# Two blocks split ahead between two layers, rows normed on two engines, and a last norm that uses TensorE

## The chip, the cores and the metric

The kernel runs on one core of one Trainium2 chip. Its engines are TensorE (PE in the profile, with weight loads as PEld), VectorE (DVE), ScalarE (ACT), GpSimd (POOL) and SyncE (SP), which here only issues DMAs. The metric is the device time of one execution in microseconds, the median of several runs. All times below are in microseconds, counted from the start of the span.

## The reference, cut to what matters

Two layers over 256 tokens of width 2048: a Mamba-2 SSD layer, then a sparse-attention layer. After each, the residual is added and the rows are normed:

```python
def layer_norm(x, g, b):
    mu = mean(x, -1); var = mean((x - mu)**2, -1)
    return (x - mu) * rsqrt(var + 1e-5) * g + b

def ssd_mixer(x, w_in, ...):
    z, xbc, dt = split(x @ w_in)            # 4096, 4096 + 2048, 64 columns
    xs, bm, cm = split(silu(conv4(xbc)))    # 8 groups of 8 heads of 64
    y = ssd(xs, dt, a, bm, cm) + d_skip * xs
    yg = rms_norm_per_group(y * silu(z)) * norm_g
    return yg @ w_out

def dsa_mixer(x, w_in, ...):
    c_q, c_kv, k_idx, w_idx, gate = split(x @ w_in)   # 512, 256, 64, 16, 4096
    ...                                               # index scores, top 64, attention
    return (o * silu(gate)) @ w_out

x = layer_norm(4**0.25 * x + ssd_mixer(x), ln_g[0], ln_b[0])
x = layer_norm(4**0.25 * x + dsa_mixer(x), ln_g[1], ln_b[1])
```

## The kernel before

All weights stream from memory in 404 blocks of 128 x 1024 (eight of them 128 x 672). For each block, SyncE loads it into one of four `raw` buffers, ScalarE copies it to a rounded high part `hi` (L98), VectorE subtracts to get the low part `lo` (L106), and TensorE uses both, so that a product of full accuracy is made of fast reduced-precision passes. The class `Stream` (L65) keeps this list: `run` (L120) goes through the blocks, splits up to `SPLIT` = 4 blocks ahead (`convert_to`, L115), issues the block's products and then lets every running side job take one step (a job is a Python generator, a `yield` ends its step). `st.limit` caps how far ahead is split. `convert` with `later=True` (by way of `start`, L109) issues only ScalarE's high part; `finish` (L104) issues the low part and the load of the block four places on. Nothing reorders this: each engine works in the order in which the program issues to it, and waits by semaphores.

The first layer's input projection is 160 blocks, 20 for each of 8 groups; the last eight of a group make its four z tiles, each summed out of PSUM by `halves` (L289: ScalarE copies one half, VectorE adds the other, in two steps of a job) and gated in `z_steps` (L324). The sums take three PSUM buffers in turn (`acc_tile`), and the two halves of the first output block `o1_0` take the next two of them. `xst_steps` (L382) transposes a pair of x tiles on TensorE. Then the output projection follows: 64 blocks (`out_proj`, L495), block column by block column; of the last one the products of the second token half are held back for six blocks, and `tail1` (L997) places them.

Between the layers, for each half of 128 tokens: `residual` (L546) adds and takes statistics on VectorE, `normed` (L953) gets the mean and the inverse root in small steps (`rsqrt1_steps`, L201) and norms four quarters of 512 columns in place, `turn` (L975) transposes a quarter on TensorE, `put` (L982) scales it by gain and bias on ScalarE and splits it into `x1T`, which the next layer's first blocks (`wcq`, `stream_tok`, L630) read. Here `n_o1` is the first of those blocks; eight of them also hold back their second token half, and `early` (L1027) makes the second half's turns and puts behind the sixth and the seventh. `AHEAD` (L55) is how many of the new layer's blocks may be split before `tail1`.

At the end, `last` (L1094) places the held products of the final output block (their last 256 columns in `part`), then `residual2` and `normed2(0)` for the first token half, then the same for the second half: mean and root, and for each quarter `center` (subtract the mean, times the gain), `scale` (times the root, plus the bias) and a write to the output by SyncE.

Of the kernel before, what the change touches and what calls it, by code (L numbers as in the profile page):

```python
# [9 lines left out]
F32 = mybir.dt.float32  # L10
# [6 lines left out]
P = 128  # L17
# [34 lines left out]
EARLY = 8  # L52
HELD = 6
LAST = 8
AHEAD = 4  # L55


class Unit:
# [78 lines left out]
def trunk_kernel(ctx: ExitStack, tc: tile.TileContext, x, xt, w1, wdt, dtp, prm, wo1,  # L137
# [23 lines left out]
    def m_tile(name):  # L161
        return p_m.tile([P, 512], F32, tag="m", name=name)
# [48 lines left out]
    def now(gen):  # L211
        for _ in gen:
            pass
# [72 lines left out]
                                         skip_group_check=True)  # L286
        return pe

    def halves(dst, ps):  # L289
        nc.scalar.activation(dst, ps[:, T:2 * T], AF.Copy)  # L290
        yield
        v.tensor_add(dst, ps[:, 0:T], dst)  # L292
        yield

# [29 lines left out]
    def z_steps(g, ci, cell):  # L324
        ps = cell["ps"]
        zs = sp2.tile([P, T], F32, tag="zs", name=f"zs{g}_{ci}", bufs=4)
        yield from halves(zs, ps)
        th = sp3.tile([P, T], F32, tag="craw", name=f"zt{g}_{ci}")
        nc.scalar.activation(th, zs, AF.Tanh, scale=0.5)
        yield  # L330
        v.scalar_tensor_tensor(zs, th, 1.0, zs, op0=ALU.add, op1=ALU.mult)
        G[g][("z", ci)] = zs
        yield
# [226 lines left out]
    for g in range(NG):  # L560
        u = 20 * g
        gap = 5 if g < 7 else 2
        st.side(u + 9, (cb_steps, g))
        st.side(u + 13, (xst_steps, g, 0))
        st.side(u + 18, (xst_steps, g, 1))
        for c in range(4):
            st.side(max(u + 5 + gap * c, 9 + c), (abc_steps, g, c))
            st.side(u + 13 + gap * c, (m_steps, g, c))
            if c % 2:
                st.side(u + 18 + max(gap * c, 2 * c), (y_steps, g, c // 2))  # L570
        if g % 2:
            st.side(u + 18 + gap * 3 + 7, (norm_steps, g // 2))
# [380 lines left out]
    def normed(half, between=()):  # L953
        mv, rs, steps = ln_stats(half)
        for step in between:
            next(step, None)
            next(steps, None)
        now(steps)
        for step in between:
            now(step)  # L960
        if half == 0:
            for n in range(4):
                s = L["r"][:, half, n * 512:(n + 1) * 512]
                v.tensor_scalar(s, s, mv[:, 0:1], rs, op0=ALU.subtract, op1=ALU.mult)
            return
        nm = d1.tile([P, 1], F32, tag="nm", name="nm")
        v.scalar_tensor_tensor(nm, mv[:, 0:1], -1.0, rs, op0=ALU.mult, op1=ALU.mult)
        for n in range(4):
            s = L["r"][:, half, n * 512:(n + 1) * 512]
            if n % 2:  # L970
                nc.scalar.activation(s, s, AF.Identity, scale=rs, bias=nm)
            else:
                v.tensor_scalar(s, s, mv[:, 0:1], rs, op0=ALU.subtract, op1=ALU.mult)
# [21 lines left out]
        v.tensor_sub(lo, t, hi.bitcast(F32))  # L995

    def tail1(cell, held, mm):  # L997
        now(residual(3, 0, cell))
        normed(0)
        X1.append(big.tile([P, KT, 2 * T], F32R, tag="B", name="x1T"))  # L1000
        xcell[0] = X1[0]
        for a in held[:4]:
            mm(*a, 1)
        turn(0, 0)
        turn(0, 1)
        mm(*held[4], 1)
        turn(0, 2)
        turn(0, 3)
        mm(*held[5], 1)
        st.limit = n_o1 + EARLY + 2  # L1010
        st.convert_to(n_o1 + AHEAD)
        now(put(0, 0))
        now(put(0, 1))
        st.convert_to(n_o1 + AHEAD + 1)
        now(residual(3, 1, cell))
        st.convert_to(n_o1 + 6)
        p2, p3 = put(0, 2), put(0, 3)

        def split():
            st.start(n_o1 + 6)  # L1020
            st.start(n_o1 + 7)
            yield
            st.finish(n_o1 + 6, v)
        normed(1, (p2, p2, p3, p3, split()))
        st.finish(n_o1 + 7, v)

    def early(kb):  # L1027
        if kb == 6:
            turn(1, 0)
            turn(1, 1)  # L1030
            now(put(1, 0))
            now(put(1, 1))
        elif kb == 7:
            turn(1, 2)
            turn(1, 3)
            now(put(1, 2))
            now(put(1, 3))
            st.convert_to(n_o1 + EARLY + 2)
    L.update(tail1=tail1, early=early)
    st.run(n_o1)  # L1040
    st.drain()
# [52 lines left out]
    def last(cell, held, mm):  # L1094
# [24 lines left out]
        def normed2(half):  # L1119
            mv, rs, steps = mean(half)  # L1120
            for n in range(4):
                next(steps, None)
                next(steps, None)
                center(half, n, mv)
            now(steps)
            for n in range(4):
                scale(half, n, rs)

        part = m_tile("part")
        k = len(held) - 4  # L1130
        for a in held[:k]:
# [4 lines left out]
            mm(*a, 1, part=part[:, 0:256], cols=(256, 512), first=held[k][1])  # L1136
        c3 = r[:, 1, 1536:2048]

        now(residual2(3, 0, cell))
        normed2(0)  # L1140
        v.scalar_tensor_tensor(c3, c3, ALPHA, cell["ps"][1], op0=ALU.mult, op1=ALU.add)
        v.bn_stats(sts[:, 1, 6, :], c3[:, 0:256])
        v.tensor_add(c3[:, 256:512], c3[:, 256:512], part[:, 0:256])
        v.bn_stats(sts[:, 1, 7, :], c3[:, 256:512])
        normed2(1)
    L["tail2"] = last

    st.run(n_heads)
# [93 lines left out]
```

## Time and profile before

| | |
|---|---|
| time, median of 3 runs | 1250.34 (1250.04 to 1251.18) |
| the profiled execution: its time, its span | 1250.64, 1248.9 |
| TensorE busy (products) | 1229.4 (98%) |
| VectorE, ScalarE, GpSimd busy | 924.0 (74%), 696.2 (56%), 67.9 (5%) |
| granted TensorE clock, mean | 0.997 |

The span is the time between the first and the last instruction of the program in the profile; the rest of the execution's time lies around it. Busy time of TensorE is modelled from issue to end, and products overlap: their spacing, from start to start, says how fast it goes. The line numbers are those of the kernel before.

### The profile page before, as it was taken

What the parts mean: (1) busy time and instruction counts of PE and PEld (TensorE: products, weight loads), DVE (VectorE), ACT (ScalarE), POOL (GpSimd) and SP (SyncE); (2) the same over time, 40 slices, a digit from 0 to 9 for tenths busy, and PEclk for the clock granted to TensorE, in tenths of its full rate; (3) what the DMA queues carried; (4) which work ended last, traced back from release to release, by engine and by line L of the source; (5) the groups of instructions that cost most, each with busy time, mean ns of one, the idle gap of its engine ahead of it and who ended that gap; (6) DMA issues with size and microseconds to landing.
All of it is one profiled execution on the core that took longest, in us unless ns stands there. A gap on an engine that the chain in (4) does not pass through costs nothing.

```text
span 1248.9 us, 19259 instructions
## 1 busy us (share of the span) xinstructions
PE 1229.4 (98%) x7098; PEld 1069.2 (86%) x7098; DVE 924.0 (74%) x1722; ACT 696.2 (56%) x1236; POOL 67.9 (5%) x104
## 2 busy tenths in 40 slices
PE   8999999999999999999999999999999999999996
PEld 6888888888888888788887898999999999888885
DVE  6978788898898889756557668866767666667457
ACT  5566565666656666544335655566666666443440
POOL 1001001100110011110000000000000000000000
PEclk9999999999999999999999999999999999999998
DMA  8666667576656665677666564544444444965652
GB/s 276 210 191 184 204 181 211 156 217 177 214 170 206 184 211 165 190 234 225 195 192 197 194 205 146 189 155 151 154 152 153 151 153 155 349 207 186 201 200 85
DMA packets 65293, 236.53 MB, mean 189 GB/s; under 512 B 7912, under 2 KB 7920, under 8 KB 64816
## 3 DMA queue, kind: packets, MB, share of 16 engines
q1 hardware_dynamic: 60192, 215.12, 54.1%
q0 software_dynamic: 5008, 20.19, 5.1%
q8 instruction: 56, 0.92, 0.3%
q14 instruction: 37, 0.30, 0.1%
HBM read 231.00 MB, written 4.28 MB: 188 GB/s over the span
## 4 chain that ended last, share of the span: by engine, by line
PE 90%; DVE 6%; ACT 2%; issue 1%; DMA 1%; DVEq 0%; SPq 0%; ACTq 0%
PE acc L285 20%; PE acc L282 10%; PE g L285 9%; PE o L511 9%; PE o L513 9%; PE o L512 9%; PE g L282 5%; DVE lo L106 2%; PE y L409 2%; PE q L843 1%; PE q L845 1%; PE q L844 1%; PE lg L873 1%; PE pt L897 1%; DVE ca L311 1%
## 5 line engine op out<-in xcount | busy, mean ns | idle before, releaser
L106 DVE TENSOR_TENSOR lo<-raw,hi 128x1024 fp32r<-128x1024 f32 (+1 forms) x404 | 489.7, 1214 | 260.9 <-ACT hi L98 259.8
L98 ACT ACTIVATE hi<-raw 128x1024 fp32r<-128x1024 f32 (+1 forms) x404 | 421.4, 1049 | 218.3 <-PE o L513 158.6
L285 PE MATMUL acc<-xT,hi 128*128 128x512 f32 x1280 | 314.2, 394 | 0.0
L285 PEld LDWEIGHTS acc<-xT,hi 128*128 128x128 f32 x1280 | 233.4, 188 | 45.7 <-ACT E L364 0.9
L282 PEld LDWEIGHTS acc<-xT,lo 128*128 128x128 f32 x1280 | 164.5, 191 | 6.4
L282 PE MATMUL acc<-xT,lo 128*128 128x256 f32 x1280 | 167.9, 283 | 0.0
L285 PE MATMUL g<-x1T,hi 128*128 128x512 f32 x512 | 130.4, 398 | 0.0
L285 PEld LDWEIGHTS g<-x1T,hi 128*128 128x128 f32 x512 | 92.7, 188 | 17.5
L511 PE MATMUL o<-hi,yg 128*128 128x512 f32 x256 | 100.5, 393 | 0.8 <-DVE zs L292 0.8
L513 PE MATMUL o<-hi,yg 128*128 128x512 f32 x256 | 99.7, 389 | 0.0
L512 PE MATMUL o<-lo,yg 128*128 128x512 f32 x256 | 99.6, 389 | 0.0
L511 PE MATMUL o<-hi,og 128*128 128x512 f32 (+1 forms) x256 | 99.4, 388 | 0.0
L513 PE MATMUL o<-hi,og 128*128 128x512 f32 (+1 forms) x256 | 98.9, 386 | 0.0
L512 PE MATMUL o<-lo,og 128*128 128x512 f32 (+1 forms) x256 | 98.8, 386 | 0.0
L282 PE MATMUL g<-x1T,lo 128*128 128x256 f32 x512 | 73.4, 288 | 0.0
L311 DVE SCALAR_TENSOR_TENSOR ca<-cr,convh,ca 128x255 f32<-128x255 f32 x144 | 69.2, 481 | 3.4
L282 PEld LDWEIGHTS g<-x1T,lo 128*128 128x128 f32 x512 | 67.7, 190 | 3.2
L314 ACT ACTIVATE cr<-ca 128x256 f32<-128x256 f32 x48 | 20.1, 418 | 88.6 <-DVE ca L311 88.6
L511 PEld LDWEIGHTS o<-hi,yg 128*128 128x128 f32 x256 | 48.0, 188 | 11.4 <-ACT hi L98 1.4
L513 PEld LDWEIGHTS o<-hi,yg 128*128 128x128 f32 x256 | 48.0, 188 | 10.0
L512 PEld LDWEIGHTS o<-lo,yg 128*128 128x128 f32 x256 | 48.1, 188 | 9.8
L512 PEld LDWEIGHTS o<-lo,og 128*128 128x128 f32 x256 | 48.1, 188 | 9.6
(252 smaller groups left out, 1735.0 us busy)
## 6 DMA issues: line engine op xcount, KB each, us to landing
raw<-in_w_dram SPq DMA_DIRECT2D x160, 512.0 KB, 4.1
raw<-in_wo_dram SPq DMA_DIRECT2D x128, 512.0 KB, 4.3
raw<-in_wg_dram SPq DMA_DIRECT2D x64, 512.0 KB, 3.3
raw<-in_wab_dram SPq DMA_DIRECT2D x32, 512.0 KB, 3.2
abc<-acs_d POOLq DMA_DIRECT2D x32, 256.0 KB, 4.4
raw<-in_wcq_dram SPq DMA_DIRECT2D x8, 512.0 KB, 4.5
raw<-in_wkv_dram SPq DMA_DIRECT2D x8, 336.0 KB, 3.2
rx<-in_x_dram POOLq DMA_DIRECT2D x2, 1024.0 KB, 11.3
```

The lines of the kernel that those rows point to most:

```text
L98: self.nc.scalar.activation(h[:, :w], r[:, :w], AF.Copy)
L106: eng.tensor_sub(*self.halfway.pop(i))
L282: nc.tensor.matmul(ps[:, 0:T], l[:, w], xs[:, kt, 0:T], start=False, stop=last, skip_group_check=True)
L285: nc.tensor.matmul(ps, h[:, w], xs[:, kt, :], start=(kt == 0), stop=last, skip_group_check=True)
L311: v.scalar_tensor_tensor(acc[:, d:], rw[:, :T - d], w(k), acc[:, d:], op0=ALU.mult, op1=ALU.add)
L314: nc.scalar.activation(rw, acc, AF.Tanh)
L409: nc.tensor.matmul(py[ks, c * T + s * P:(c + 1) * T], xsT[:, s, c, ks], ms[c][k][:, ws], start=(c == 0 and s == 0), stop=(s == 1), skip_gr ...
L511: nc.tensor.matmul(ps, ah, hs, start=(kk == 2 * first), stop=False)
L512: nc.tensor.matmul(ps, ah, ls, start=False, stop=False)
L513: nc.tensor.matmul(ps, al, hs, start=False, stop=(kk == 31))
L843: nc.tensor.matmul(ps, h[:, o:o + P], cqT[:, kt, 0:T], start=(kt == 0), stop=False)
L844: nc.tensor.matmul(ps, h[:, o:o + P], cqT[:, kt, T:2 * T], start=False, stop=False)
```

## The change

Five edits.

- The last two z tiles are summed in one step: `halves` gets a flag, and without its `yield` the add on VectorE is issued right behind ScalarE's copy.
- The transposes of the last pair of x tiles are issued one block later.
- Between the layers, `AHEAD` goes from 4 to 2. Of blocks n_o1+2 and n_o1+3 only the high parts are issued ahead of the first half's residual, the low parts behind its norm. Blocks n_o1+8 and n_o1+9 are split behind the second half's last put, not ahead of its norm.
- `normed` treats both halves alike: quarters 0 and 2 on VectorE, quarters 1 and 3 on ScalarE, the negated product of mean and root between the first two.
- In the last norm of the second half, three quarters are multiplied by the gain early. When the mean is known, ScalarE scales a negated identity by it, and TensorE forms row times gain minus mean times gain in three PSUM buffers (`c0` to `c2`): one product with the identity, one with the scaled identity each. VectorE centers and scales only the fourth quarter, and finishes the other three by one operation each, times the root plus the bias.

```diff
--- before.py
+++ after.py
@@ -52,7 +52,7 @@
 EARLY = 8
 HELD = 6
 LAST = 8
-AHEAD = 4
+AHEAD = 2
 
 
 class Unit:
@@ -286,9 +286,10 @@
                                          skip_group_check=True)
         return pe
 
-    def halves(dst, ps):
+    def halves(dst, ps, wait=True):
         nc.scalar.activation(dst, ps[:, T:2 * T], AF.Copy)
-        yield
+        if wait:
+            yield
         v.tensor_add(dst, ps[:, 0:T], dst)
         yield
 
@@ -324,7 +325,7 @@
     def z_steps(g, ci, cell):
         ps = cell["ps"]
         zs = sp2.tile([P, T], F32, tag="zs", name=f"zs{g}_{ci}", bufs=4)
-        yield from halves(zs, ps)
+        yield from halves(zs, ps, wait=g * 4 + ci < NG * 4 - 2)
         th = sp3.tile([P, T], F32, tag="craw", name=f"zt{g}_{ci}")
         nc.scalar.activation(th, zs, AF.Tanh, scale=0.5)
         yield
@@ -562,7 +563,7 @@
         gap = 5 if g < 7 else 2
         st.side(u + 9, (cb_steps, g))
         st.side(u + 13, (xst_steps, g, 0))
-        st.side(u + 18, (xst_steps, g, 1))
+        st.side(u + 18 + (g == NG - 1), (xst_steps, g, 1))
         for c in range(4):
             st.side(max(u + 5 + gap * c, 9 + c), (abc_steps, g, c))
             st.side(u + 13 + gap * c, (m_steps, g, c))
@@ -958,14 +959,10 @@
         now(steps)
         for step in between:
             now(step)
-        if half == 0:
-            for n in range(4):
-                s = L["r"][:, half, n * 512:(n + 1) * 512]
-                v.tensor_scalar(s, s, mv[:, 0:1], rs, op0=ALU.subtract, op1=ALU.mult)
-            return
-        nm = d1.tile([P, 1], F32, tag="nm", name="nm")
-        v.scalar_tensor_tensor(nm, mv[:, 0:1], -1.0, rs, op0=ALU.mult, op1=ALU.mult)
+        nm = d1.tile([P, 1], F32, tag=f"nm{half}", name=f"nm{half}")
         for n in range(4):
+            if n == 1:
+                v.scalar_tensor_tensor(nm, mv[:, 0:1], -1.0, rs, op0=ALU.mult, op1=ALU.mult)
             s = L["r"][:, half, n * 512:(n + 1) * 512]
             if n % 2:
                 nc.scalar.activation(s, s, AF.Identity, scale=rs, bias=nm)
@@ -995,6 +992,8 @@
         v.tensor_sub(lo, t, hi.bitcast(F32))
 
     def tail1(cell, held, mm):
+        st.start(n_o1 + 2)
+        st.start(n_o1 + 3)
         now(residual(3, 0, cell))
         normed(0)
         X1.append(big.tile([P, KT, 2 * T], F32R, tag="B", name="x1T"))
@@ -1007,11 +1006,12 @@
         turn(0, 2)
         turn(0, 3)
         mm(*held[5], 1)
-        st.limit = n_o1 + EARLY + 2
-        st.convert_to(n_o1 + AHEAD)
+        st.limit = n_o1 + EARLY
+        st.finish(n_o1 + 2, v)
+        st.finish(n_o1 + 3, v)
         now(put(0, 0))
         now(put(0, 1))
-        st.convert_to(n_o1 + AHEAD + 1)
+        st.convert_to(n_o1 + 5)
         now(residual(3, 1, cell))
         st.convert_to(n_o1 + 6)
         p2, p3 = put(0, 2), put(0, 3)
@@ -1035,7 +1035,8 @@
             turn(1, 3)
             now(put(1, 2))
             now(put(1, 3))
-            st.convert_to(n_o1 + EARLY + 2)
+            st.limit = n_o1 + EARLY + 2
+            st.convert_to(st.limit)
     L.update(tail1=tail1, early=early)
     st.run(n_o1)
     st.drain()
@@ -1126,6 +1127,29 @@
             for n in range(4):
                 scale(half, n, rs)
 
+        def scaled(n):
+
+            s, g, _ = cut(1, n)
+            v.tensor_mul(s, s, g)
+            sums[n] = acc_tile(f"c{n}")
+
+        def normed2b():
+            mv, rs, steps = mean(1)
+            neg = d1.tile([P, P], F32, tag="neg", name="neg")
+            nc.scalar.activation(neg, nident, AF.Copy, scale=mv[:, 0:1])
+            for n in range(3):
+                nc.tensor.matmul(sums[n], ident, cut(1, n)[0], start=True, stop=False)
+            for n in range(3):
+                nc.tensor.matmul(sums[n], neg, cut(1, n)[1], start=False, stop=True)
+            now(steps)
+            center(1, 3, mv)
+            scale(1, 3, rs)
+            for n in range(3):
+                s, _, b = cut(1, n)
+                v.scalar_tensor_tensor(s, sums[n], rs, b, op0=ALU.mult, op1=ALU.add)
+                nc.sync.dma_start(out[P:2 * P, n * 512:(n + 1) * 512], s)
+
+        sums = {}
         part = m_tile("part")
         k = len(held) - 4
         for a in held[:k]:
@@ -1136,13 +1160,17 @@
             mm(*a, 1, part=part[:, 0:256], cols=(256, 512), first=held[k][1])
         c3 = r[:, 1, 1536:2048]
 
+        for n in range(3):
+            scaled(n)
         now(residual2(3, 0, cell))
         normed2(0)
+        nident = d1.tile([P, P], F32, tag="nident", name="nident")
+        nc.scalar.activation(nident, ident, AF.Copy, scale=-1.0)
         v.scalar_tensor_tensor(c3, c3, ALPHA, cell["ps"][1], op0=ALU.mult, op1=ALU.add)
         v.bn_stats(sts[:, 1, 6, :], c3[:, 0:256])
         v.tensor_add(c3[:, 256:512], c3[:, 256:512], part[:, 0:256])
         v.bn_stats(sts[:, 1, 7, :], c3[:, 256:512])
-        normed2(1)
+        normed2b()
     L["tail2"] = last
 
     st.run(n_heads)
```

On VectorE, at the end of the first input projection, this stood before (`lo161` and `lo162` are low parts of the first output blocks, `zs7_2` the last but one z tile, `acc156` its PSUM buffer):

```order
L377 TENSOR_TENSOR M59_5459<-E59_5395,cbm7_5206 128x384
L366 TENSOR_SCALAR E61_5466<-abc60_5167,ask_118 128x256
L366 TENSOR_SCALAR E61_5466<-abc60_5167,ask_118 128x128
L106 TENSOR_TENSOR lo161_5470<-raw161_5321,hi161_5469 128x1024
L466 TENSOR_TENSOR yg1_531<-yf20_5342,yg1_531 128x256
L473 SCALAR_TENSOR_TENSOR yf22_5494<-xs5_2_3978,par_88,rbs2_4945 128x256
L331 SCALAR_TENSOR_TENSOR zs7_1_5390<-zt7_1_5455,zs7_1_5390 128x256
L292 TENSOR_TENSOR zs7_2_5461<-acc156_5404,zs7_2_5461 128x256
L106 TENSOR_TENSOR lo162_5507<-raw162_5361,hi162_5506 128x1024
L377 TENSOR_TENSOR M60_5532<-E60_5463,cbm7_5206 128x384
```

And this stands now:

```order
L378 TENSOR_TENSOR M59_5459<-E59_5395,cbm7_5206 128x384
L293 TENSOR_TENSOR zs7_2_5461<-acc156_5404,zs7_2_5461 128x256
L367 TENSOR_SCALAR E61_5467<-abc60_5167,ask_118 128x256
L367 TENSOR_SCALAR E61_5467<-abc60_5167,ask_118 128x128
L106 TENSOR_TENSOR lo161_5471<-raw161_5321,hi161_5470 128x1024
L467 TENSOR_TENSOR yg1_531<-yf20_5342,yg1_531 128x256
L474 SCALAR_TENSOR_TENSOR yf22_5495<-xs5_2_3978,par_88,rbs2_4945 128x256
L332 SCALAR_TENSOR_TENSOR zs7_1_5390<-zt7_1_5455,zs7_1_5390 128x256
L106 TENSOR_TENSOR lo162_5503<-raw162_5361,hi162_5502 128x1024
L332 SCALAR_TENSOR_TENSOR zs7_2_5461<-zt7_2_5498,zs7_2_5461 128x256
```

The sum of `zs7_2` has moved up by six places, ahead of the low part `lo161`.

On VectorE between the layers, before (`lo224` is the low part of block n_o1, `rx` the residual rows, `o1_3_0` the last output sums of the first half):

```order
L106 TENSOR_TENSOR lo224_6777<-raw224_6726,hi224_6776 128x1024
L106 TENSOR_TENSOR lo225_6789<-raw225_6744,hi225_6788 128x1024
L106 TENSOR_TENSOR lo226_6801<-raw226_6756,hi226_6800 128x1024
L549 SCALAR_TENSOR_TENSOR rx_6155<-rx_6155,o1_3_0_6564 128x512
L552 BN_STATS st1_6156<-rx_6155 128x6 x2
L624 BN_AGGR mv0_6815<-st1_6156 128x2
```

Now:

```order
L106 TENSOR_TENSOR lo224_6777<-raw224_6726,hi224_6776 128x1024
L106 TENSOR_TENSOR lo225_6789<-raw225_6744,hi225_6788 128x1024
L550 SCALAR_TENSOR_TENSOR rx_6155<-rx_6155,o1_3_0_6564 128x512
L553 BN_STATS st1_6156<-rx_6155 128x6 x2
L625 BN_AGGR mv0_6815<-st1_6156 128x2
```

and, some steps on, where the first half's norm ends:

```order
L209 SCALAR_TENSOR_TENSOR rs0_6816<-t0_6818,rs0_6816 128x1
L970 TENSOR_SCALAR rx_6155<-rx_6155,mv0_6815,rs0_6816 128x512
L965 SCALAR_TENSOR_TENSOR nm0_6828<-mv0_6815,rs0_6816 128x1
L970 TENSOR_SCALAR rx_6155<-rx_6155,mv0_6815,rs0_6816 128x512
L106 TENSOR_TENSOR lo226_6807<-raw226_6756,hi226_6806 128x1024
L106 TENSOR_TENSOR lo227_6810<-raw227_6768,hi227_6809 128x1024
L988 CAST x1T_6834<-rx_6155 128x4x128
```

The low part `lo226` (n_o1+2) has moved from ahead of the residual to behind the norm; two of four quarters are left on VectorE, with `nm0` between them.

On ScalarE at the second half's norm, before (`x1t10` to `x1t13` are its transposed quarters, `hi232` and `hi233` the high parts of n_o1+8 and n_o1+9):

```order
L98 ACTIVATE hi231_6947<-raw231_6893 128x1024
L971 ACTIVATE rx_6155<-rx_6155,nm_6956,rs1_6923 128x512 x2
L98 ACTIVATE hi232_7006<-raw232_6911 128x672
L98 ACTIVATE hi233_7018<-raw233_6920 128x672
L987 ACTIVATE rx_6155<-x1t10_7030,par_88 128x128 x4
```

Now:

```order
L98 ACTIVATE hi231_6949<-raw231_6895 128x1024
L968 ACTIVATE rx_6155<-rx_6155,nm1_6958,rs1_6925 128x512 x2
L984 ACTIVATE rx_6155<-x1t10_7020,par_88 128x128 x4
L984 ACTIVATE rx_6155<-x1t11_7025,par_88 128x128 x4
L984 ACTIVATE rx_6155<-x1t12_7048,par_88 128x128 x4
L990 ACTIVATE x1T_6834<-rx_6155 128x4x128
L984 ACTIVATE rx_6155<-x1t13_7053,par_88 128x128 x4
L990 ACTIVATE x1T_6834<-rx_6155 128x4x128
L98 ACTIVATE hi232_7070<-raw232_6913 128x672
```

The two high parts have moved from ahead of the evictions of the transposed quarters to behind them.

## Rows read from the trace of the kernel before

**Rows 1.** The page, part 1: TensorE busy, share, instructions.
```profile
PE 1229.4 (98%) x7098; PEld 1069.2 (86%) x7098; DVE 924.0 (74%) x1722; ACT 696.2 (56%) x1236; POOL 67.9 (5%) x104
```

**Rows 2.** Timeline, TensorE, input projection ends: start, us, instruction, [idle before].
```profile
496.06 0.38 PE L389 MATMUL pxs<-ident,xs 128*128 128x128 f32 x2
...
496.81 0.44 PE L389 MATMUL pxs<-ident,xs 128*128 128x128 f32 x2 [0.36 <-DVE xs L320]
...
501.45 0.40 PE L513 MATMUL o<-hi,yg 128*128 128x512 f32 x1
...
502.63 0.47 PE L511 MATMUL o<-hi,yg 128*128 128x512 f32 x1 [0.78 <-DVE zs L292]
```

**Rows 3.** Timeline of VectorE (DVE) in the same stretch.
```profile
498.48 1.01 DVE L377 TENSOR_TENSOR M<-E,cbm 128x384 f32<-128x384 f32 x2
...
502.08 0.41 DVE L292 TENSOR_TENSOR zs<-acc,zs 128x256 f32<-128x256 f32 x1
```

**Rows 4.** Timeline of VectorE between the layers.
```profile
671.17 2.52 DVE L106 TENSOR_TENSOR lo<-raw,hi 128x1024 fp32r<-128x1024 f32 x2 [1.74 <-ACT hi L98]
...
673.61 0.68 DVE L549 SCALAR_TENSOR_TENSOR rx<-rx,o 128x512 f32<-128x512 f32 x1
...
675.11 0.37 DVE L624 BATCH_NORM_AGGREGATE mv<-st 128x2 f32<-128x48 f32 x1
...
677.21 0.16 DVE L209 SCALAR_TENSOR_TENSOR rs<-t,rs 128x1 f32<-128x1 f32 x1
...
677.40 1.00 DVE L964 TENSOR_SCALAR rx<-rx,mv,rs 128x512 f32<-128x512 f32 x2
...
689.48 1.23 DVE L106 TENSOR_TENSOR lo<-raw,hi 128x1024 fp32r<-128x1024 f32 x1
```

**Rows 5.** Timeline of TensorE between the layers.
```profile
676.34 0.39 PE L513 MATMUL o<-hi,yg 128*128 128x512 f32 x1
...
678.00 1.11 PE L979 MATMUL x1t<-ident,rx 128*128 128x128 f32 x8 [1.28 <-DVE rx L964]
...
678.87 0.47 PE L511 MATMUL o<-hi,yg 128*128 128x512 f32 x1
...
679.18 0.39 PE L512 MATMUL o<-lo,yg 128*128 128x512 f32 x1
...
690.99 0.39 PE L640 MATMUL qp<-lo,x1T 128*128 128x512 f32 x1
...
694.38 1.04 PE L979 MATMUL x1t<-ident,rx 128*128 128x128 f32 x8
...
696.61 0.39 PE L639 MATMUL qp<-hi,x1T 128*128 128x512 f32 x1
```

**Rows 6.** Timeline of ScalarE (ACT) between the layers.
```profile
678.70 2.91 ACT L987 ACTIVATE rx<-x1t,par 128x128 f32<-128x128 f32 x8 [5.01 <-PE x1t L979]
...
690.81 0.82 ACT L971 ACTIVATE rx<-rx,nm,rs 128x512 f32<-128x512 f32 x1 [1.29 <-DVE nm L967]
...
692.23 1.41 ACT L98 ACTIVATE hi<-raw 128x672 fp32r<-128x672 f32 x2
```

**Rows 7.** Timeline of VectorE in the last norm.
```profile
1226.25 0.69 DVE L943 SCALAR_TENSOR_TENSOR fin<-fin,o 128x512 f32<-128x512 f32 x1 [3.04 <-PE o L513]
...
1238.35 0.37 DVE L1101 BATCH_NORM_AGGREGATE mv<-st 128x2 f32<-128x48 f32 x1
...
1242.80 2.74 DVE L1115 SCALAR_TENSOR_TENSOR fin<-fin,rs 128x512 f32<-128x512 f32 x4
```

**Rows 8.** Timeline of TensorE: first products, a full-precision one in two passes, the last.
```profile
7.87 1.64 PE L592 MATMUL p_dt<-scr 128*64 128x256 f32 x3
...
468.30 0.59 PE L338 MATMUL cb<-C,B 128*128 128x256 f32 x2
...
1237.12 0.28 PE L513 MATMUL part<-hi,og 128*128 128x256 f32 x1
```

**Rows 9.** A window at the end: PE, PEld, DVE, ACT, POOL busy, granted clock, DMA.
```profile
1241.00:1243.00 2.00, 0.00 (x0) 0.00 (x0) 1.96 (x7) 0.00 (x0) 0.00 (x0) 0.70 0.00 0
```

## The prediction

> **What bounds the kernel now.** I read the page's engine table first: TensorE (PE) is busy almost all the time [rows 1]. So an edit can only pay in two ways: it closes a stretch in which TensorE has nothing to do, or it shortens what runs after TensorE's last product. I then went through TensorE's timeline for starts that come later than the spacing of the products around them. Past the first loads there are three places, and a tail:
>
> - The end of the first input projection [rows 2]. The two transposes at 496.06 are spaced 0.11 (eight of them take 0.87 from 678.00 to 678.87, rows 5), so the next two could have started at 496.28; they start at 496.81, after the last x tile. The first half of the first output block ends with a product at 501.45, its successor could start 0.23 later, at 501.68; it starts at 502.63, when VectorE (DVE) has summed a z tile out of the PSUM buffer that the second half needs. Lost: 0.53 + 0.95.
> - Between the layers [rows 5]. After the product at 676.34 TensorE runs dry at 676.57; the first transpose of the normed rows starts at 678.00.
> - Still between the layers: transposes of the second token half start at 694.38 and are issued by 695.25. With the restart spacing seen behind the first set (678.87 to 679.18) and 0.23 after it, the fourth product would start at 696.02; it starts at 696.61. Lost: 0.59.
> - The tail: TensorE issues its last product at 1237.12 [rows 8], VectorE finishes the last row block at 1245.54 (1242.80 + 2.74, rows 7), and the writes and the program's end follow.
>
> Elsewhere the blocks are split well ahead of TensorE and no row shows it starting late, so time won at one place should be kept to the end.
>
> **Part A, the z tiles and the transposes.** No work is added. The sum of the last but one z tile moves on VectorE from behind the next block's split and two gating products to directly behind the M products that end at 499.49 [rows 3]. It is 0.41 long, so the PSUM buffer is free at about 499.8, while TensorE, 0.53 earlier by then, wants it at 501.15. The four transposes move behind the last projection product and the `ms` product, where their x tile is long written. They take the same 0.44 there. Their reader on VectorE moves down in its queue too; its consumer, the second set of y products, comes several blocks later, and those blocks cover it. The sequence on VectorE keeps its length. **A = 0.53 + 0.95 = 1.48.**
>
> **Part B, between the layers.** Before, VectorE makes two low parts in a row from 671.17 to 673.69, 1.23 each, and only then the residual of the first half, at 673.61 [rows 4]. Now the second of them stands behind the normalization. The residual waits only for the first, so it starts near 672.32: 1.29 earlier, and the statistics with it. The first quarter, still on VectorE, starts at 677.40 - 1.29 = 676.11. Before, the first transpose came 0.60 after that start, so now 676.71, only 0.14 after TensorE runs dry.
>
> But the second quarter is now ScalarE's. VectorE spends about half of the 1.00 that two quarters take, 0.46, on the first one, then makes the negated mean, a one-column operation of 0.15 like the root's last step (0.16), until 676.72; ScalarE starts 0.04 later and takes 0.82 (its norming of the second half, rows 6), until 677.58. The second four transposes thus start at about 677.63, not right behind the first four, end 0.44 later, and the held products go on at 678.07 where they went on at 678.87. Of 1.29 that VectorE gains, 0.80 reaches TensorE; the rest is a new wait for ScalarE. **B1 = 0.80.**
>
> What else moves here: the low parts of blocks n_o1+2 and n_o1+3 now end near 678.3 and 679.5, and TensorE wants the first of them only behind two held blocks, two more transposed quarters (0.44 each) and two block halves of the new layer (six products of 0.23 each, 1.36), after 684. The load that the moved step issues on SyncE (block n_o1+6) now goes out near 678.3, some 4.6 later; the low part of that block is made at 689.48 [rows 4], so more than 10 us stay for its landing and its high part. The loads behind it in the queue wait for later splits anyway. VectorE's later chain gains only about 0.5, because it follows ScalarE's evictions: these started at 678.70 [rows 6], and now two normings of at most 0.82 stand ahead of them, from 676.76 to about 678.2. That eats margins: the low part of n_o1+6 ends at 690.71 and its product starts at 690.99 [rows 5]; 0.8 earlier against 0.5 earlier leaves the two level. I take nothing off for it, and it is the next thing to be late.
>
> The second half: ScalarE makes two block splits (1.41, rows 6) before the evictions of the second half. These two go behind them now. The evictions come 1.4 earlier, TensorE's need 0.8 earlier, so the 0.59 goes. The two splits are wanted only after the eight second halves, some 10 us later. **B2 = 0.59.**
>
> **Part C, the end.** Three products of row and gain (three operations of a 512-column row, at most 0.68 each like the last ones in rows 7, 2.05 together) are put ahead of the first half's last residual. VectorE is idle there for 3.04 before 1226.25 [rows 7], so they cost nothing; without that cover they would cost their 2.05.
>
> At the end, four centerings are replaced by one. The mean stands at 1238.35; by the between-layer chain the last step of the root starts 2.10 after the mean (675.11 to 677.21, rows 4), at 1240.45; the one centering can follow 0.07 later and ends near 1241.26, its scaling near 1241.98, and then three combining operations at about 0.66 spacing end at 1243.90. Before it was 1245.54: **C = 1.64**, if TensorE's sums are there in time. The writes follow as before.
>
> Are they? Six products of 512 full-precision columns are not in the trace. Nearest rows: a 256-column one is two passes in 0.59, the first's own length 0.38 [rows 8], so 0.21 a pass and 0.43 for 512 columns: twelve passes, 5.16, from 1237.24 to 1242.4, the result some 0.16 later. The last combining operation starts at 1243.22, so 0.6 is spare. The negated identity needs the mean (1238.72), then one small ScalarE operation (under 0.5, shorter than the 0.82 of a 512-column row); TensorE wants it at 1239.8. Other bound: three such passes among the program's first products take 1.64 [rows 8], so at most 0.55 for 256 columns and 1.09 for 512. I take 0.43, since TensorE has been at work up to that point, as it had for the 0.59; the other end is a rival.
>
> The combining operation reads PSUM. The row of such an operation, at 1226.25, lasts 0.69 [rows 7], and four that read SBUF alone take 2.74, so 0.68 each; I add nothing. [...]
>
> **Sum.** 1.48 + 0.80 + 0.59 + 1.64 = 4.51 from the profiled execution's 1250.64: 1246.13. The median shown is 0.30 below that execution, so **1245.8**.
>
> **Rivals.**
>
> *The new waits eat part B.* For it: the level margins above, and the wait for ScalarE that I already had to charge. Against: each is a few tenths. If half of B goes, 0.7 is lost: 1246.5.
>
> *Part C brings nothing.* TensorE's six products come later than VectorE wants them; at 0.62 a pass the last operation would end where it ended before. For it: no such product is in the trace. Against: the nearest row of a warmed-up TensorE gives 0.43. A and B alone leave 1250.34 - 2.87 = 1247.5.
>
> *Slower: TensorE's clock falls under the tail products.* Its place is the twelve passes. [...] At twice 0.43 a pass twelve take 10.3, VectorE ends 2.9 later than before, and the whole change is worth nothing: 0.86 is the point from which it is a loss. At the other bound, 1.09, the passes end at 1250.3 and VectorE at 1251.2, 5.6 later than before; less 2.87 of A and B that is 1253.1. Against: here the products follow the last block without a stop, and the only wait on the way (for the negated identity) has 0.6 to spare. [...]
>
> *It does not do what it says*: if the block landing ahead of the first low part (VectorE idles 1.74 before 671.17, rows 4) comes later, B1 shrinks. That is inside the first rival.
>
> **Numbers.** Forecast 0.70 (own range 1245.1 to 1246.6), half of B lost 0.14, C nothing 0.12, slower 0.04. A measurement tells about 0.2% (2.5 us) from no change, so faster means below 1247.8. All of the first two cases but 0.02 and half of the third lie below that: 0.88. The same: 0.09. Slower: 0.03. Range 1244.9 to 1247.6: the lower end takes in the case that ScalarE's quarter does not hold up the transposes (0.5 more) and an error of some tenths in each term; the upper end reaches the case in which C brings nothing.
>
> **What would show it.** In the profile after: no idle time ahead of the second output half, nor of the transposes in the projection; the first residual starts right behind one low part; a short idle stretch between the first and the second four transposes, put down to ScalarE; the fourth product of the second half spaced like its neighbours; twelve passes of about 0.43 behind the last block; three combining operations of 0.68 without a wait for TensorE, and VectorE done some 6.7 after TensorE's last block product (8.3 before). It is wrong if the combining operations wait for TensorE, or if some other start of TensorE comes late by what was won.

## The result, and the profile after

The changed kernel takes 1244.04 us (median of 6 runs, 1243.29 to 1244.51) where the kernel before, measured beside it, takes 1250.57 (6 runs, 1250.04 to 1251.18): ratio 0.9947, 95% interval 0.9934 to 0.996. It is faster, as forecast, but by 6.5 us instead of 4.5, and 1244.04 lies 0.9 below the lower end of the range. The profiled executions say the same: 1244.22 with a span of 1242.5, against 1250.64 with 1248.9.

The page after, part 1, TensorE's busy time, share and instructions [rows 1]: the share is up to 99%.

```profile
PE 1231.7 (99%) x7110; PEld 1069.3 (86%) x7110; DVE 923.0 (74%) x1721; ACT 697.4 (56%) x1240; POOL 68.0 (5%) x104
```

TensorE's timeline at the end of the input projection [rows 2]: the four transposes now stand behind the projection, and the second output half (501.62) follows at the normal spacing of 0.23. Both stops are gone.

```profile
499.80 0.60 PE L390 MATMUL pxs<-ident,xs 128*128 128x128 f32 x4
...
501.39 0.39 PE L514 MATMUL o<-hi,yg 128*128 128x512 f32 x1
501.62 0.40 PE L512 MATMUL o<-hi,yg 128*128 128x512 f32 x1
```

VectorE there [rows 3]: the sum of the z tile follows the M products directly.

```profile
498.98 1.01 DVE L378 TENSOR_TENSOR M<-E,cbm 128x384 f32<-128x384 f32 x2
499.92 0.41 DVE L293 TENSOR_TENSOR zs<-acc,zs 128x256 f32<-128x256 f32 x1
```

VectorE between the layers [rows 4]: one low part instead of two ahead of the residual (671.04), then two quarters of the rows at 674.84 and 675.37 with the negated mean between them.

```profile
669.90 1.23 DVE L106 TENSOR_TENSOR lo<-raw,hi 128x1024 fp32r<-128x1024 f32 x1 [1.66 <-ACT hi L98]
671.04 0.68 DVE L550 SCALAR_TENSOR_TENSOR rx<-rx,o 128x512 f32<-128x512 f32 x1
...
674.84 0.55 DVE L970 TENSOR_SCALAR rx<-rx,mv,rs 128x512 f32<-128x512 f32 x1
675.30 0.15 DVE L965 SCALAR_TENSOR_TENSOR nm<-mv,rs 128x1 f32<-128x1 f32 x1
675.37 0.54 DVE L970 TENSOR_SCALAR rx<-rx,mv,rs 128x512 f32<-128x512 f32 x1
```

ScalarE there [rows 6]: its two quarters take 1.52 together.

```profile
675.49 1.52 ACT L968 ACTIVATE rx<-rx,nm,rs 128x512 f32<-128x512 f32 x2 [2.10 <-DVE nm L965]
```

TensorE there [rows 5]: no stop before the first four transposes (675.59), 0.17 before the second four, put down to ScalarE; the held products go on at 676.77, and the fourth product behind the second half's transposes starts at 694.08.

```profile
675.36 0.40 PE L514 MATMUL o<-hi,yg 128*128 128x512 f32 x1
675.59 0.60 PE L976 MATMUL x1t<-ident,rx 128*128 128x128 f32 x4
676.36 0.66 PE L976 MATMUL x1t<-ident,rx 128*128 128x128 f32 x4 [0.17 <-ACT rx L968]
676.77 0.48 PE L512 MATMUL o<-hi,yg 128*128 128x512 f32 x1
...
692.51 1.04 PE L976 MATMUL x1t<-ident,rx 128*128 128x128 f32 x8
...
694.08 0.39 PE L640 MATMUL qp<-hi,x1T 128*128 128x512 f32 x1
```

The tail on TensorE [rows 8]: the last block product starts at 1232.20; twelve passes follow without a stop, six in 2.74, so (2.74 - 0.59)/5 = 0.43 apart.

```profile
1232.20 0.29 PE L514 MATMUL part<-hi,og 128*128 128x256 f32 x1
1232.33 2.74 PE L1141 MATMUL c<-fin,ident 128*128 128x512 f32 x6
1234.90 2.74 PE L1143 MATMUL c<-fin,neg 128*128 128x512 f32 x6
```

The window from 1232 to 1238; the last column but two is the granted clock, 1.00:

```profile
1232.00:1238.00 6.00, 5.64 (x17) 2.42 (x15) 5.09 (x15) 0.40 (x1) 0.00 (x0) 1.00 0.00 0
```

And on VectorE [rows 7]: the mean at 1233.44, one centering, one scaling, three combining operations, done at 1239.13.

```profile
1227.40 2.73 DVE L1116 SCALAR_TENSOR_TENSOR fin<-fin,rs 128x512 f32<-128x512 f32 x4
...
1233.44 0.37 DVE L1102 BATCH_NORM_AGGREGATE mv<-st 128x2 f32<-128x48 f32 x1
...
1235.62 0.74 DVE L1112 SCALAR_TENSOR_TENSOR fin<-fin,mv 128x512 f32<-128x512 f32 x1
1236.40 0.75 DVE L1116 SCALAR_TENSOR_TENSOR fin<-fin,rs 128x512 f32<-128x512 f32 x1
1237.07 2.06 DVE L1149 SCALAR_TENSOR_TENSOR fin<-c,rs,fin 128x512 f32<-128x512 f32 x3
```

**Where the 6.4 us of the profiles come from.** I matched the products of the two traces one by one and took the difference of their starts along the run. Negative is earlier:

| up to | start before, after | difference | gained in this stretch |
|---|---|---|---|
| first product of the projection | 14.54, 15.05 | +0.51 | -0.51 (the first load landed 0.31 later in this execution, at 5.60; the rest was lost among the first products) |
| second output half, A done | 502.63, 501.62 | -1.01 | 1.52 |
| fourth product of the second half, B done | 696.61, 694.08 | -2.53 | 1.52 |
| end of the heads, 1068 | 1067.95, 1063.09 | -4.86 | **2.33** |
| last block product | 1237.12, 1232.20 | -4.92 | 0.06 |
| VectorE's end, C done | 1245.54, 1239.13 | -6.41 | 1.49 |

The rows at the end of the heads, before:

```profile
1067.95 0.39 PE L512 MATMUL o<-lo,og 128*128 128x512 f32 x1
```

After:

```profile
1063.09 0.39 PE L513 MATMUL o<-lo,og 128*128 128x512 f32 x1
```

A, B and C come to 4.53, against 4.51 forecast. The 2.33 between 696 and 1068 are not in the forecast: no edit touches an instruction there, and neither trace has a stop. The gain creeps in without a jump, a few ns a product. A window view of the products that read cqT (the second layer's compressed queries, first line) and ckvT (its compressed keys and values, second line) shows it. Columns: window, its length, TensorE's busy time in them (count), granted clock, DMA share, GB/s. Before:

```profile
680.00:1060.00 380.00, 62.36 (x480) 1.00 0.49 162
...
680.00:1060.00 380.00, 50.09 (x384) 1.00 0.49 162
```

After:

```profile
680.00:1060.00 380.00, 61.05 (x480) 1.00 0.49 166
...
680.00:1060.00 380.00, 49.25 (x384) 1.00 0.49 166
```

The same number of products, the same full clock, 1.31 + 0.84 = 2.15 us less. The starts tell it too: these 256-column products stood 120 ns apart, now mostly 117. At the same time the gates' 256-column products, which stream x1T, stay at 120.

What differs between the two programs for cqT and ckvT is their place. A pool is a stretch of the on-chip memory, and the program lays the pools out one behind the other. The two 128x128 tiles of the new last norm (`neg`, `nident`, 512 bytes per partition each) and the second mean (a slot of 32) are tiles of pool `d1`, and the pools that are opened after it lie behind it. By the programs' allocation ckvT moves from byte 170432 to 171488 of each partition and cqT from 174528 to 175584: 1056 further. The four `hi` and `lo` buffers of the weights and x1T lie ahead of `d1` and stay; extra weight buffers behind it move.

### The profile page after: what moved, and what is told of

Its sections match the earlier page's. It is cut to its first block, busy times and chain, and to the rows that moved or that the text cites. A ratio compares the mean times of both kernels' runs of the same rounds, so it can differ in the third digit from the quotient of the medians.

```text
span 1242.5 us, 19284 instructions
## 1 busy us (share of the span) xinstructions
PE 1231.7 (99%) x7110; PEld 1069.3 (86%) x7110; DVE 923.0 (74%) x1721; ACT 697.4 (56%) x1240; POOL 68.0 (5%) x104
## 4 chain that ended last, share of the span: by engine, by line
PE 96%; DVE 2%; DMA 1%; issue 0%; ACT 0%; DVEq 0%; SPq 0%
PE acc L285 23%; PE acc L282 12%; PE g L285 10%; PE o L512 9%; PE o L514 9%; PE o L513 9%; PE g L282 5%; PE y L410 2%; PE q L844 1%; PE q L845 1%; PE q L846 1%; PE lg L874 1%; DVE lo L106 1%; PE pt L898 1%; PE p_dt L593 1%; PE pxs L390 1%
## 5 line engine op out<-in xcount | busy, mean ns | idle before, releaser
L514 PEld LDWEIGHTS o<-hi,og 128*128 128x128 f32 x256 | 48.1, 188 | 9.9
```

What stands on the lines that cost most here:

```text
L514: nc.tensor.matmul(ps, al, hs, start=False, stop=(kk == 31))
```

## The experiments

"Place" is my theory that TensorE's rate on these products hangs on where in the partition the tiles begin. Ratios are to the kernel before on the same chip, with 95% intervals.

**1. Only the place, on the kernel before.** Pads of 32 and of 1024 bytes at the head of `d1`:

```
     d1 = ctx.enter_context(tc.tile_pool(name="d1", bufs=1))
+    d1.tile([P, 8], F32, tag="pad", name="pad")      # second run: [P, 256]
```

> The kernel before with one unused tile of 32 bytes per partition at the head of pool d1: every tile of the pools opened after it (ckvT, cqT, the heads' tiles, the extra weight buffers) starts 32 bytes further on, so no longer at a multiple of 64; no instruction is added, removed or moved. Theory 'place' (the 256-column products read faster where a tile starts 32 beyond a multiple of 64): q, k, v and index products go from 120 to about 117 ns apart, 2.45 us gained between 700 and 1070, some 0.5 lost again in about 88 products of 512 columns that read the shifted weight buffers (233 instead of 227 ns): 1248.6 us. Rival 'distance' (it was the kilobyte, another memory bank): no change, 1250.6. Rival 'order' (it comes of the changed instruction stream, whatever the addresses): no change, 1250.6.

> The kernel before with an unused tile of 1024 bytes per partition at the head of pool d1: the same tiles move by 1024 and still start at multiples of 64. 'Place': no change, 1250.6 us, spacing 120 ns. 'Distance': the gain seen after the change, spacing 117 ns, 1248.6. 'Order': no change, 1250.6.

Measured: 32 bytes 1248.46 us, 0.9979 (0.997 to 0.9988); 1024 bytes 1250.78, 0.9999 (0.999 to 1.0008). Not one instruction differs from the kernel before, and 32 bytes give what the changed kernel has in this stage, to the digit. The same view, 32 bytes:

```profile
680.00:1060.00 380.00, 61.05 (x480) 1.00 0.47 164
...
680.00:1060.00 380.00, 49.25 (x384) 1.00 0.47 164
```

1024 bytes:

```profile
680.00:1060.00 380.00, 62.36 (x480) 1.00 0.46 162
...
680.00:1060.00 380.00, 50.09 (x384) 1.00 0.46 162
```

So it is the place; "order" and "distance" fall. Of the 1056 bytes the 32 do it. The memory bank in "distance" was a guess of mine; no run shows one.

**2. The changed kernel with its tiles at home, and a split version.**

```
-        nm = d1.tile([P, 1], F32, tag=f"nm{half}", name=f"nm{half}")
+        nm = nms[:, half:half + 1]       # nms: one tile [P, 2] in d1
...
-            neg = d1.tile([P, P], F32, tag="neg", name="neg")      # nident likewise
+            neg = dt.tile([P, P], F32, tag="neg", name="neg")      # dt: opened last
...
     # split version, also:
+    lat.tile([P, 8], F32, tag="pad", name="pad")      # ahead of ckvT
```

> The changed kernel with the two 128x128 tiles of the last norm in a pool of their own behind all others and the two means in one small tile, so that ckvT, cqT, the heads' tiles and the extra weight buffers stand at the addresses that they had before the change; the same instructions in the same order. 'Place' and 'distance': the head products are back at 120 ns and about 2 us of the gain goes: 1246.0 us, which is what the prediction's own terms sum to (1245.8). 'Order': 1244.0 as the changed kernel.

> The changed kernel with ckvT, cqT and the heads' tiles 32 beyond a multiple of 64, as in the changed kernel, but the six extra weight buffers of the output projection and of the start of the second layer back at multiples of 64. 'Place', with the opposite sign for 512 columns: head products at 117 ns, the 512-column products that read these buffers back from 233 to 227: 0.3 to 0.5 faster than the changed kernel, 1243.6 us. 'Distance': 1246.0, since nothing is moved by a kilobyte. 'Order': 1244.0.

Measured: at home 1245.99 us, 0.9964 (0.9951 to 0.9976); its window lines read 62.36 and 50.09 again. That is 0.2 from the forecast of 1245.8, but the interval, 3.0 to 6.1 us of gain, is wide and overlaps that of the changed kernel, so the trace decides. From the fourth product of the second half to the end of the heads it has these two rows:

```profile
694.71 0.39 PE L640 MATMUL qp<-hi,x1T 128*128 128x512 f32 x1
...
1066.04 0.39 PE L513 MATMUL o<-lo,og 128*128 128x512 f32 x1
```

The stretch takes 371.33, where it took 371.34 before (696.61 to 1067.95) and takes 369.01 in the changed kernel (694.08 to 1063.09): all of the 2.33 is gone again. The split version: 1243.16, 0.9941 (0.9928 to 0.9953), the fastest kernel here by its median, although its interval overlaps that of the changed kernel. What it adds shows in the trace: the first products of the second layer stream 512 columns out of the six extra weight buffers, which the changed kernel also moves off their place. By line, from 680 to 706 (mean ns of one behind the busy time), changed kernel:

```profile
L641 PE MATMUL qp<-lo,x1T 128*128 128x512 f32 x32 | 12.6, 393 | 0.0
```

Split version:

```profile
L641 PE MATMUL qp<-lo,x1T 128*128 128x512 f32 x32 | 12.5, 390 | 0.0
```

By the starts, 512-column products from a moved buffer stand about 233 ns apart, from one at home 227. So the same shift that speeds up 256 columns slows down 512.

**3. The three parts alone**, each on the kernel before, all tiles at home; the edits are those of the diff.

> Part A alone on the kernel before (the sum of the last two z tiles without a pause, the last four transposes of the projection one block later); all tiles at the addresses of before. The prediction's term: TensorE's stops of 0.4 to 0.5 us before the transposes at 497 and of 0.8 to 0.95 us in the first output block vanish, 1.48 us gained: 1249.1 against a kernel before of 1250.6. Rival 'given back': the time won at 502 is lost again before 678, because the low parts and the residual there do not come earlier than before; then TensorE's stop ahead of the transposes at 678 grows by as much and the time is 1250.6.

> Part B alone on the kernel before (two blocks split ahead, rows normed on two engines, the later limit), the two means in one small tile, all tiles at the addresses of before. The prediction's terms: 0.80 at the first half's transposes and 0.59 in the second half, 1.39 together: 1249.2 against 1250.6. Rival 'half of it lost' to the wait for ScalarE's quarter: 1249.9, with TensorE idle before the second four transposes. Rival 'A and B share a gain' (each alone brings more than its part of the two): under 1248.8.

> Part C alone on the kernel before (the last half's norm with TensorE's products), the two 128x128 tiles in a pool behind all others, all tiles at the addresses of before. The prediction's term: VectorE ends 6.7 us after TensorE's last block product instead of 8.4, twelve passes 0.43 apart: 1.64 gained, 1248.9 against 1250.6. Rival 'a slower root': the trace of the changed kernel has 6.9 instead of 6.7, so 1.5: 1249.1. Rival 'clock': passes 0.86 apart and no gain, 1250.6.

Measured, beside a kernel before of 1250.92: A 1249.43, 0.9988 (0.9979 to 0.9997), so 1.49 gained against 1.48; B 1249.16, 0.9988 (0.9979 to 0.9997), 1.76 against 1.39; C 1249.58, 0.999 (0.9981 to 0.9999), 1.34 against 1.64. Together 4.59. The intervals reach about a microsecond to either side, so they show that each part pays, not its tenths; the traces are sharper.

A's gain is kept: the stop ahead of the transposes is 1.25 long where it was 1.28 [rows 5], so nothing is given back there.

```profile
677.14 1.11 PE L980 MATMUL x1t<-ident,rx 128*128 128x128 f32 x8 [1.25 <-DVE rx L965]
```

B alone closes that stop altogether: eight transposes in one go, no wait for ScalarE, 1.30 earlier than before, and the fourth product of the second half at 694.60, 2.01 earlier. So "half of it lost" is out. "A and B share a gain" is settled by the traces too: counted from the projection's first product, the fourth product of the second half comes 1.70 earlier with A alone, 2.17 with B alone, and 3.74 in the split version, which has both. They add up within 0.2.

```profile
676.70 1.04 PE L976 MATMUL x1t<-ident,rx 128*128 128x128 f32 x8
...
694.60 0.39 PE L639 MATMUL qp<-hi,x1T 128*128 128x512 f32 x1
```

C alone repeats the tail: the last block product starts at 1237.57, VectorE ends at 1242.43 + 2.06 = 1244.49, 6.92 later (8.42 before, [rows 7, 8]).

```profile
1237.57 0.28 PE L513 MATMUL part<-hi,og 128*128 128x256 f32 x1
```

```profile
1242.43 2.06 DVE L1148 SCALAR_TENSOR_TENSOR fin<-c,rs,fin 128x512 f32<-128x512 f32 x3
```

**4. Which places?** First, the split version with ckvT 16 and cqT 48 bytes off their places of before (each tile 8 elements longer, used from element 4). The heads' tiles behind them stand 96 bytes off, where the split version has 32, so the time has that in it too:

> The kernel of the split experiment (heads' tiles at 32, extra weight buffers at multiples of 64), but ckvT starts 16 bytes and cqT 48 bytes beyond a multiple of 64. Theory 'any start off the multiple of 64': k, v (ckvT) and q, index products (cqT) stay 117 ns apart, 1243.2 us. Rival 'only the half line of 32': both at 120 ns, 1245.5. Rival 'starts that are no multiple of 32 cost an access more': over 120 ns, each ns on some 750 products 0.75 us, 1246 and more.

Measured 1245.16, 0.9955 (0.9942 to 0.9968): between the theories. That a half line or one access more decides was a guess of mine; no run shows either.

```profile
680.00:1060.00 380.00, 61.70 (x480) 1.00 0.48 165
...
680.00:1060.00 380.00, 49.53 (x384) 1.00 0.48 165
```

Then pads of 64, 96 and 160 bytes on the kernel before, by the same edit as in 1:

> The kernel before with an unused tile of 64 bytes per partition at the head of pool d1. Before, ckvT and cqT start 64 bytes beyond a multiple of 128, as do the weight tiles; here they start at a multiple of 128. Theory 'period of 128' (read together with the run at 16 and 48: 117 ns only where the moving tile starts at 96 of 128, near 120 at 32 and 64): q, k, index products stay at 120 ns, 1250.8 us. Rival 'any distance to the weights' start that is not 0 within 128': 117 ns, 1248.4.

> The kernel before with an unused tile of 96 bytes at the head of pool d1: ckvT and cqT start at 32 of 128. 'Period of 64' (my reading after the first four runs): 117 ns, 1248.5 us. 'Period of 128': about 120 ns as in the 256-column products of the last blocks in the run at 16 and 48, and 0.5 lost in the 512-column products of the shifted weight buffers: 1251.2.

> The kernel before with an unused tile of 160 bytes at the head of pool d1: ckvT and cqT start at 96 of 128 as in the run with 32 bytes, but at 96 of 512 where that one has 480 of 512. 'Period of 128': 117 ns, 1248.5 us. 'Period of 256 or 512' (the good place is 32 below such a multiple): 120 ns, 1251.2.

Measured: 64 bytes 1248.89, 0.9981 (0.9971 to 0.999); 96 bytes 1250.92 and 160 bytes 1250.82, both 0.9997 (0.9988 to 1.0006). My "period of 128" got 96 right, which gains nothing, and missed the other two: 64 gains and 160 does not. "Period of 64" missed at 96. In the order 64, 96, 160:

```profile
680.00:1060.00 380.00, 61.23 (x480) 1.00 0.48 164
...
680.00:1060.00 380.00, 48.70 (x384) 1.00 0.48 164
```

```profile
680.00:1060.00 380.00, 62.43 (x480) 1.00 0.47 162
...
680.00:1060.00 380.00, 49.77 (x384) 1.00 0.47 162
```

```profile
680.00:1060.00 380.00, 61.82 (x480) 1.00 0.47 162
...
680.00:1060.00 380.00, 49.95 (x384) 1.00 0.47 162
```

No rule by multiples of 64 or 128 fits. 0 and 1024 agree, and so do 32 and 1056: a pattern that repeats after 1024 bytes would fit, and these runs show no shorter one.

**5. Places picked from these spacings.** The v products, which load ckvT as weights, were 114 ns apart with the pad of 64, so I put ckvT and the weights' low parts 64 off their places of before, with pads behind them so that all else keeps its place within 512 bytes:

```
+    pads.tile([P, 16], F32, tag="pad", name="pad")      # a pool ahead of wlo
     wlo = ctx.enter_context(tc.tile_pool(name="wlo", bufs=SPLIT))
...
+    pads.tile([P, 112], F32, tag="pad", name="pad")     # another pool, behind wlo
...
+    lat.tile([P, 16], F32, tag="pad", name="pad")
     ckvT = lat.tile([P, 2, 2 * T], F32R, tag="ckvT", name="ckvT")
+    lat.tile([P, 120], F32, tag="pad2", name="pad2")
```

> The kernel of the split experiment with two more places chosen from the spacings measured so far: the low parts of the weights (pool wlo) and ckvT start 64 bytes further on (a multiple of 512 instead of 448 of 512), cqT and the heads' tiles as there, all else at its place within 512 bytes; no instruction is changed. Theory 'the start of the tile that is loaded as weights counts as well': v products, whose weights are ckvT, were 114.4 ns apart in the run with 64 bytes and 118.2 in the one with 32, so 192 of them gain 0.7 us; the 256-column products of the input projection and of the gates, whose weights are low parts, go from 119.4 and 119.0 to about 114.4, some 1570 products by 4 to 5 ns: 6 to 8 us; the 512-column products of both output projections that stream low parts lose about 1 ns each, 0.5 us. Sum: 1235.5 to 1237.5 us against 1243.2 of the split kernel. Rival 'only the streamed tile counts': 1243.0. Rival 'VectorE becomes the bound in the input projection': the lo products 114 ns apart, but TensorE then waits for VectorE there and the time stays above 1240.

Measured 1248.43, 0.9977 (0.9968 to 0.9986): some 5 us slower than the split version. The projection's 256-column products do go to 118 ns (from its first product, 14.51 and now 14.19, to the first output product, 499.63 and now 497.16, it takes 2.15 less; from 60 to 480 its 2214 products are busy for 392.39, where in the split version as many are for 394.60), but the output projections lose more. TensorE's products that read `og`, from 1080 to 1200, split version and then this one:

```profile
1080.00:1200.00 120.00, 119.68 (x529) 1.00 0.59 201
```

```profile
1080.00:1200.00 120.00, 119.68 (x517) 1.00 0.58 197
```

That is 226 and 231 ns a product. I had charged 1 ns, and only on those that stream a low part; the hi products beside them, whose tiles had not moved, lost as much (a mean of 227 in the split version, 232 here). So the spacing of a product does not hang on one tile, nor on its own two alone: where the tiles of the products beside it lie counts as well. And the v products did not come to 114, they are 118.5 apart, also those that stream a `hi` tile at its old address, with ckvT at the same place within 512 bytes as with the pad of 64. Whether that is the low parts beside them or the 512 bytes, no run shows.

## Why the prediction was wrong, and where it was right

- **The step that failed** is a term that the sum did not have: "Elsewhere the blocks are split well ahead of TensorE and no row shows it starting late, so time won at one place should be kept to the end." The time won was kept; but I took the stretch from 697 to 1068 as unchanged because its instructions are unchanged. I had read the diff's new tiles as free memory. They move every tile behind them, and that was worth 2.33 where the sum has nothing: 2.15 us of busy time in the cqT and ckvT products, the rest among the other products of the heads. With the tiles at home the stretch takes its old time, 371.33 for 371.34, and the kernel 1245.99 for the 1245.8 forecast. This was shown by changing the place alone (32 bytes, no other edit) and by undoing the place alone.
- **A** was right: 1.52 in the changed kernel's trace, 1.49 alone, for 1.48.
- **B** came to 1.52 for 1.39, nearer than its parts, which is luck: errors of opposite sign met. B1 was 1.09, not 0.80 (held products at 678.87 and 676.77: 2.10, less A's 1.01). The residual was 2.57 earlier, so 1.56 beyond A's share where I had 1.29, and ScalarE's two quarters take 1.52 together where I had 0.82 for one. The forecast wait for ScalarE is there, 0.17. B2 was 0.66 (696.61 to 694.08 against 694.38 to 692.51) for 0.59. Between the two, 0.23 was lost again: the 512-column products from the moved buffers, for which the sum had no term either. In the split version, without that, and in B alone the waits are gone; how long the first is hangs on when the load of the block ahead of the low part lands (in the changed kernel ScalarE waits 1.82 for it before the high part at 668.80), and that differed between the executions traced (the low part starts at 669.90 in the changed kernel, at 668.10 in the split version), so B1 has an uncertainty of some tenths.
- **C** was 1.49 for 1.64: VectorE ends 6.93 after the last block product starts, where before it was 8.42 (the prediction's closing list says 8.3, its own rows 8.42). Twelve passes at 0.43 as taken, the granted clock at 1.00 from 1232 to 1238 (before, with TensorE idle, it averaged 0.70 from 1241 to 1243 [rows 9]), and the combining operations wait for nothing: the third starts at 1238.39, the last pass ends at 1237.64. The 0.15 went in VectorE's own steps, 5.69 from the mean's start to the end where I had 5.55. The slower rival, which needed 0.86 a pass, is out: no run shows passes at twice 0.43, neither the changed kernel nor C alone (six in 2.74 in both). I had added nothing for an operand in PSUM, and that was right: three combining operations out of PSUM start (2.06 - 0.74)/2 = 0.66 apart, four out of SBUF (2.73 - 0.74)/3 = 0.66, and a single one lasts 0.74 to 0.75 of either kind.
- **The range** was built from the waits' uncertainties. None of my cases had the unchanged stages change, so its lower end, 1244.9, could not hold it.

## What to carry to other kernels

When an edit adds, drops or resizes a tile, look at what lies behind it in the allocation: here 2 to 3 ns on each of 864 unchanged products came to 2.15 us, more than A or B brought (1.52 each). A comparison of two schedules is clean only with the tiles of the untouched stages at their old addresses: of the 6.4 us here 2.33 came of the addresses. And where a kernel is bound by TensorE, as this one is (busy for 98% of the span), a pad of 32 or 64 bytes is worth a trial (here ratios of 0.9979 and 0.9981), with the spacing of every kind of product read from the trace, since what helps 256 columns can cost 512: here 117 ns for 120, but 233 for 227.

## What the runs showed of the hardware

- The spacing of f32r products on TensorE (the reduced-precision passes) at a granted clock of 1.00 depends on the start of the tiles within the partition: 114 to 120 ns for 256 columns (120 before, 117 with the pad of 32, 114 for the v products with the pad of 64), 227 to 233 for 512 (227 from buffers at home, 233 from those that the changed kernel moves). It repeats from run to run: the same places give 62.36 and 50.09 us, or 61.05 and 49.25, to the digit in different kernels.
- Open: the rule, and the reason behind it. It is not the multiple of 64 (the pad of 64 takes 1248.89 us, no pad 1250.57) or of 128 (the pad of 32 takes 1248.46, that of 160 takes 1250.82). The streamed tile counts (the q products, of which cqT alone moved, go from 120 to 117), the tile loaded as weights counts (the projection's 256-column products, of which the low part alone moved, from 120 to 118), the tiles of the neighbouring products count (the hi products of the output projections, from 227 to 232), and with the places tried here 256 and 512 columns want different ones: 32 further on 256 columns go from 120 to 117 and 512 from 227 to 233; with the low parts 64 further on, from 120 to 118 and from 226 to 231.
